# Twelve weight differences on GpSimd and four changes of order in the second attention group of a hybrid layer

## The chip, the core and the metric

The kernel runs on one core of a Trainium2 chip. The metric is the device time of one execution in microseconds (us). The engines are TensorE (PE, matmuls and transposes into PSUM), VectorE (DVE), ScalarE (ACT), GpSimd (POOL) and SyncE (SP, which here only issues DMAs). Each engine works its own queue in order; the queues meet through semaphores.

## What is computed

A layer over 1024 tokens of width 1024, in float32:

```
hn = rmsnorm(x);  proj = hn @ w_in                  # queries, keys, values of two groups
o_a = window attention, 8 query heads, 2 kv heads, |i-j| <= 128, a learned sink per head
o_b = neighbourhood attention on a 16 x 64 grid, 8 heads, window 8 x 16, learned bias
h  = x + concat(rmsnorm(o_a), rmsnorm(o_b)) @ w_out
hn = rmsnorm(h)
g  = conv3(hn @ w_gate) + conv_b;  u = hn @ w_up    # hidden width 2816
out = rmsnorm(h + (silu(g) * u) @ w_down)
```

## The kernel before, in words

**Arithmetic.** Every float32 operand of a matmul is split in two parts that TensorE takes at one pass each: a high part, made by an ACT copy, and a low part, the rest, made by a DVE subtraction. A product of a 128 x 128 weight block with 512 columns is then three matmuls: high x high, high x low, low x high (`block`, L168 to L171; `group`, L955 to L959). The weight halves are called whi and wlo, those of the probabilities ph and pl (`split_pt`, L413), those of activations hg.

**Order.** TensorE's order is written out by hand. For the other engines a scheduler takes instructions by priority, which is their place in the traced program, as far as their operands and buffers are ready in its own reckoning; the order in each queue is then fixed. `tc.high_priority(offset=n)` puts the instructions of a block n places forward. `behind(...)` (L145) keeps the instructions of a block, on the engine of the marked instruction, behind that instruction in its queue: it orders a queue and adds no wait between engines. Marks are kept in the dict `mark` and overwritten by each new instruction of that kind, so a mark means the latest one traced.

**Attention.** Projections are jobs m = 0 to 17 (`Project`, L554). They and the first half of the output projection (`OutA`, L590, eight tiles d of the four mixed tiles of group A) are fed as filler between the steps of attention units (`fill`, L805). A unit's step computes scores (L381), a softmax (L392: DVE adds the bias and takes the extreme, ACT the exp, DVE the reciprocal, POOL multiplies by it), transposes the probabilities on TensorE (pt), splits them into ph and pl and multiplies by the values (L528, L529). Group B's heads come last, and the last projection, m = 17, makes query and key of the last head. Its result is evacuated from PSUM by `evacuate` (L236, DVE), and `split_qk` (L292) makes ka on ACT and kb on DVE; four DMAs on SP then stack halves into q, kb and ka. `settle` (L725) calls this when the next job has run `LAG` = 3 blocks. `load` of the next job is traced when a job begins, `load_rest`, which makes the second half of a projection's weights, at its 12th block (`REST`). `OutA.run` first loads its tile xr of x (512 KB, SP, L604), which is added when the product leaves PSUM (L609). At the end of the attention units a dummy square root (L896) makes ACT load the table that later norms need.

**Gate and up.** Both products are computed with a Strassen-like scheme of seven products, each with its own weight combination: "11" and "12" are halves of the gate weights, "22" one of up, and s1, s2, s4, s3 are sums and differences: s1 = u1 + u2, s2 = s1 − g1, s4 = g2 − s2, s3 = g1 − u1. For the first four tiles (`HEAD` = 4, units 0 to 3, L1168 to L1217) each product is run for all four before the next: p1 and p2, p5 (s1), p6 (s2), p3 (s4), p7 (s3), p4 ("22"). Their weights are made by `head_weights` (L1000): it loads the raw weights it needs into one of three raw buffers (`load_raw`, L950, SP), forms the sum or difference into a buffer that the tile keeps through s1, s2, s4 and s3 (L998), and splits it into whi and wlo (`split_w`, L941, nine buffers each). The differences for s2, s4 and s3 go through `sub` (L996), a DVE subtraction. In the same stage DVE forms the activation combinations and their low parts (L996, L965), evacuates the products (L1108, L1115, L1119, L1132, L1137) and runs two taps of the convolution (L1126, L1127). From the fifth tile on a class `Weights` (L1043) makes the combinations, and its lines are not touched.

The parts that the change touches, and those that call them:

Of the kernel before, what the change touches and what calls it, by code (L numbers as in the profile page):

```python
# [30 lines left out]

LAG, LATE = 3, 13
FILL0, FILL1 = 22, 14
# [20 lines left out]
def hybrid_layer(tc, xT, w_first, w_in, w_out, w_gate, w_up, w_down, small, sink, rpb, consts, rope, out):  # L54
    nc = tc.nc
    with ExitStack() as ctx:
# [100 lines left out]

        def halve_w(raw):

            hi, lo = (wpool.tile([128, 4, 128], F32R, name=n, tag=n) for n in ("whi", "wlo"))  # L160
            mark["weights"] = nc.scalar.activation(hi, raw, AF.Copy)
            mark["weights low"] = nc.vector.tensor_tensor(lo, raw, f32(hi[:, :, :]), op=ALU.subtract)
            return [(hi[:, j, :], lo[:, j, :]) for j in range(4)]

        def load_w(src):
            return halve_w(fetch_w(src))

# [123 lines left out]

        def split_qk(t, urgent):  # L292

            a, b, q = big("ka", "op", F32R), big("kb", "op", F32R), big("q", "op", F32R)
            by = cst[:, K_SCALE:K_SCALE + 1]
            for h in range(2):
                with tc.high_priority(offset=urgent):
                    nc.scalar.activation(a[:, tsl(h)], t[:, tsl(h)], AF.Copy, scale=by)
                    nc.vector.scalar_tensor_tensor(b[:, tsl(h)], t[:, tsl(h)], by, f32(a[:, tsl(h)]), op0=ALU.mult, op1=ALU.subtract)
            with tc.high_priority(offset=500):  # L300
                nc.sync.dma_start(f32(q[0:64, :]), f32(a[0:64, :]))
                nc.sync.dma_start(f32(q[64:128, :]), f32(b[0:64, :]))
                nc.sync.dma_start(f32(b[0:64, :]), f32(a[64:128, :]))
                nc.sync.dma_start(f32(a[0:64, :]), f32(b[64:128, :]))
            return q, (a, b)
# [52 lines left out]
        def post(m, t):  # L358

            if m < 6:  # L360
                turn(m, t)
                stacks(m, t)
            else:
                hp, i = divmod(m - 6, 3)
                if i == 0:
                    vb[2 * hp], vb[2 * hp + 1] = split_v(t, (0, 1), lambda: done.add(m))
                else:
                    h = 2 * hp + i - 1
                    qb[h], kb[h] = split_qk(t, 500 * (m == 17))

# [21 lines left out]
        def softmax(st, j, ps, n, bias, nsink=None):  # L392
# [3 lines left out]
            with tc.high_priority(offset=50):  # L396
# [9 lines left out]
                e = n if nsink is None else n + 1  # L406
                mark["exp"] = nc.scalar.activation(p[:, j, 0:e], p[:, j, 0:e], AF.Exp, bias=nm, scale=-1.0, accum_out=sm[:, j:j + 1])  # L407
                if j == 1:
# [4 lines left out]
        def split_pt(ps, n):  # L413
            ph = apool.tile([128, HALF], F32R, name="ph", tag="ph")
            pl = apool.tile([128, HALF], F32R, name="pl", tag="pl")
            with tc.high_priority(offset=100):
                nc.scalar.activation(ph[:, 0:n], ps[:, 0:n], AF.Copy)  # L417
                nc.vector.tensor_tensor(pl[:, 0:n], ps[:, 0:n], f32(ph[:, 0:n]), op=ALU.subtract)  # L418
            return ph, pl
# [134 lines left out]
        class Project:  # L554
# [7 lines left out]
            def load_rest(self):  # L562
                self.w += halve_w(self.raw)

            def run(self):
# [7 lines left out]
                else:  # L573

                    ps = [bank("pj", "pj") for _ in range(2)]
                    for k in range(KT):
# [3 lines left out]
                        if k % 2:  # L580
                            mg[k // 2] = split(mix[k // 2], "mg", "xg")
                    for h in range(2):
                        evacuate(self.t, ps[h], h, self.grid)

# [5 lines left out]
        class OutA:  # L590
# [9 lines left out]
            def run(self):  # L600
                d = self.d
                h1[d] = big("h1", "mix" if d < 4 else "op")
                xt = tmp("xr")
                nc.sync.dma_start(xt, xT[d])  # L604
                for h in range(2):
                    ps = bank("pj", "pj")
                    yield from product(ps, self.w, mg[0:4], h)
                    with tc.high_priority(offset=500):
                        nc.vector.tensor_tensor(h1[d][:, tsl(h)], ps, xt[:, tsl(h)], op=ALU.add)  # L609
# [115 lines left out]
        def settle(age):  # L725

            for item in list(later):
                item[0] -= 1
                if item[0] <= 0:
                    later.remove(item)  # L730
                    item[1]()
            while waiting and (len(waiting) > 1 or age >= (LATE if waiting[0].m == 3 else LAG)):
                m = waiting[0].m
                if live["op"] + needs(m) > slots["op"]:
                    break
                live["op"] += needs(m)
                with behind(*["stack", "low"] * (m == 3)):
                    waiting.pop(0).post()
# [128 lines left out]
        for u in range(len(flat)):  # L867
# [26 lines left out]
            live["op"] -= 7 if u in (7, 15) else 4 if u >= 16 and u % 4 == 3 else 0  # L894
        with tc.high_priority(offset=500), behind("exp"):
            nc.scalar.activation(warm, eps, AF.Sqrt)  # L896
# [103 lines left out]
        def head_weights(i, name):  # L1000
# [4 lines left out]
            elif name == "s2":  # L1005
                g = load_raw(w_gate[f, :, 0:4], 4)
                sub(t, t, g)
            elif name == "s4":
                g = load_raw(w_gate[f, :, 4:8], 4)
                sub(t, g, t)  # L1010
            elif name == "s3":
                g, u = load_raw(w_gate[f, :, 0:4], 4), load_raw(w_up[f, :, 0:4], 4)
                sub(t, g, u)
            else:
# [550 lines left out]
```

## Time and profile before

| what | value |
|---|---|
| median of three runs | 1077.05 us (1076.45 to 1077.55) |
| the profiled execution's own time | 1077.36 us |
| its span, from the first to the last instruction | 1075.6 us |
| mean granted TensorE clock | 0.998 |
| instructions | 14910 |
| PE busy | 1063.6 us |
| DVE busy | 867.5 us |
| ACT busy | 554.9 us |
| POOL busy | 106.8 us |

The page has the busy time of each engine, the chain of work that ended last, and groups of instructions. The trace answers with the busy time in given stretches, with the instructions of an engine in order of time (start, duration, engine, line, operation, output <- inputs, and in brackets how long the engine was idle before and what ended that), and with groups of instructions of one shape. A matmul's record is longer than the step from one matmul to the next, because matmuls overlap. SPq and ACTq rows are the issuing of a DMA, not its transfer. The attention lasts to about 372 us, the second half of the output projection to about 434 us, the first four gate and up tiles to about 510 us, the other eighteen and the down projection to the end.

### The profile page before, as it was taken

The numbers are of one execution on the slowest core, as the hardware profiler recorded it, in microseconds if no ns is written. First come the engines' busy times: TensorE is split into PE (matmuls) and PEld (weight loads), VectorE is DVE, ScalarE is ACT, GpSimd is POOL, SyncE is SP. The second block draws the span as 40 slices with busy tenths as digits, with TensorE's granted clock in tenths as the row PEclk, the third lists the DMA queues.
The fourth block names the chain that finished last, engine by engine and source line by source line (L and its number), as shares of the span: only waits on it lengthen the run. The fifth ranks groups of instructions, "written<-read, shape, count | busy, mean of one in ns | idle before, by whom it ended". The sixth has DMA issues, their size and how long they took to land.

```text
span 1075.6 us, 14910 instructions
## 1 busy us (share of the span) xinstructions
PE 1063.6 (99%) x5094; PEld 889.3 (83%) x5094; DVE 867.5 (81%) x1596; ACT 554.9 (52%) x1059; POOL 106.8 (10%) x188
## 2 busy tenths in 40 slices
PE   9999999999999999999999999999999999999997
PEld 7888888888888888887788888888888888888887
DVE  7889887768888699899988877887887858987675
ACT  8457776647676545534534343442433646444451
POOL 0124332222342000000000000000000000000002
PEclk9999999999999999999999999999999999999999
DMA  7223122323235246214342232332222788766644
GB/s 278 73 74 82 38 69 60 89 69 82 75 87 159 83 152 216 79 48 158 145 159 97 96 121 79 128 107 109 98 89 98 246 293 304 269 223 219 230 153 157
DMA packets 68220, 144.94 MB, mean 135 GB/s; under 512 B 8240, under 2 KB 18736, under 8 KB 68144
## 3 DMA queue, kind: packets, MB, share of 16 engines
q1 hardware_dynamic: 57920, 118.69, 34.3%
q10 hardware_dynamic: 10224, 25.30, 6.2%
q8 instruction: 40, 0.66, 0.3%
q14 instruction: 36, 0.29, 0.1%
HBM read 103.58 MB, written 28.57 MB: 123 GB/s over the span
## 4 chain that ended last, share of the span: by engine, by line
PE 89%; DVE 8%; ACT 1%; DMA 1%; issue 1%; POOL 0%; DVEq 0%; ACTq 0%; SPq 0%; POOLq 0%
PE pj L169 8%; PE pj L170 7%; PE pj L171 7%; PE dn L957 7%; PE dn L959 7%; PE dn L958 7%; PE z L959 5%; PE z L957 5%; PE z L958 5%; PE s L381 3%; PE x L957 3%; PE x L958 3%; PE x L959 3%; PE y L959 3%; PE y L957 3%; PE y L958 3%
## 5 line engine op out<-in xcount | busy, mean ns | idle before, releaser
L946 ACT ACTIVATE whi<-ws 128x512 fp32r<-128x512 f32 (+1 forms) x100 | 60.3, 622 | 126.7 <-DVE ws L1064 82.5
L957 PE MATMUL dn<-xd,whi 128*128 128x512 f32 (+1 forms) x330 | 124.0, 376 | 0.0
L959 PE MATMUL dn<-xd,wlo 128*128 128x512 f32 (+1 forms) x330 | 123.7, 375 | 0.0
L958 PE MATMUL dn<-xd,whi 128*128 128x512 f32 (+1 forms) x330 | 123.7, 375 | 0.0
L959 PE MATMUL z<-hg,wlo 128*128 128x512 f32 x264 | 103.0, 390 | 0.7 <-DVE wlo L947 0.7
L169 PE MATMUL pj<-xgh,whi 128*128 128x512 f32 x245 | 103.2, 421 | 0.0
L957 PE MATMUL z<-hg,whi 128*128 128x512 f32 x264 | 103.0, 390 | 0.2 <-ACT whi L946 0.2
L958 PE MATMUL z<-hg,whi 128*128 128x512 f32 x264 | 102.7, 389 | 0.0
L407 ACT ACTIVATE p<-p,nm 128x385 f32<-128x385 f32 (+3 forms) x128 | 75.1, 587 | 49.3 <-DVE nm L403 48.4
L411 POOL TENSOR_SCALAR p<-p,sm 128x384 f32<-128x384 f32 (+1 forms) x128 | 79.5, 634 | 206.8 <-DVE sm L409 164.0
L171 PE MATMUL pj<-xgh,wlo 128*128 128x512 f32 x245 | 96.4, 393 | 0.0
L170 PE MATMUL pj<-xgl,whi 128*128 128x512 f32 x245 | 96.2, 393 | 0.0
L947 DVE TENSOR_TENSOR wlo<-raw,whi 128x512 fp32r<-128x512 f32 (+1 forms) x102 | 66.4, 672 | 26.1 <-ACT whi L946 25.0
L946 ACT ACTIVATE whi<-raw 128x512 fp32r<-128x512 f32 (+1 forms) x102 | 60.5, 612 | 46.0 <-DMA raw<-in_w_down_dram 19.6
L418 DVE TENSOR_TENSOR pl<-pt,ph 128x384 fp32r<-128x384 f32 (+2 forms) x108 | 63.5, 589 | 24.2 <-ACT ph L417 22.5
L947 DVE TENSOR_TENSOR wlo<-ws,whi 128x512 fp32r<-128x512 f32 (+1 forms) x100 | 67.0, 683 | 18.9 <-ACT whi L946 17.7
L1382 POOL TENSOR_TENSOR h<-h,wide 128x256 f32<-128x256 f32 (+1 forms) x6 | 5.4, 919 | 707.2 <-ACT wide L1378 707.2
L1272 ACT ACTIVATE xd<-xd 128x512 fp32r<-128x512 f32 x77 | 47.3, 626 | 47.6 <-DMA xd<-x 46.5
L959 PEld LDWEIGHTS dn<-xd,wlo 128*128 128x128 f32 x330 | 62.1, 188 | 11.2
L958 PEld LDWEIGHTS dn<-xd,whi 128*128 128x128 f32 x330 | 62.1, 188 | 11.1
L957 PEld LDWEIGHTS dn<-xd,whi 128*128 128x128 f32 x330 | 62.1, 188 | 11.1
L417 ACT ACTIVATE ph<-pt 128x384 fp32r<-128x384 f32 (+2 forms) x108 | 55.0, 512 | 30.7 <-PE pt L517 23.1
(270 smaller groups left out, 2675.8 us busy)
## 6 DMA issues: line engine op xcount, KB each, us to landing
xd<-x SPq DMA_DIRECT2D x77, 256.0 KB, 4.6
raw<-in_w_down_dram SPq DMA_DIRECT2D x72, 256.0 KB, 4.0
raw<-in_w_gate_dram SPq DMA_DIRECT2D x22, 512.0 KB, 3.6
raw<-in_w_up_dram SPq DMA_DIRECT2D x22, 512.0 KB, 4.3
x<-c ACTq DMA_DIRECT2D x22, 512.0 KB, 3.6
raw<-in_w_in_dram SPq DMA_DIRECT2D x30, 256.0 KB, 2.7
raw<-in_w_down_dram SPq DMA_DIRECT2D x36, 192.0 KB, 4.6
x<-t ACTq DMA_DIRECT2D x11, 512.0 KB, 2.7
```

The lines of the kernel that those rows point to most:

```text
L169: nc.tensor.matmul(ps, w[0], x[0][:, tsl(h)], start=first, stop=False)
L170: nc.tensor.matmul(ps, w[0], x[1][:, tsl(h)], start=False, stop=False)
L171: nc.tensor.matmul(ps, w[1], x[0][:, tsl(h)], start=False, stop=last)
L407: mark["exp"] = nc.scalar.activation(p[:, j, 0:e], p[:, j, 0:e], AF.Exp, bias=nm, scale=-1.0, accum_out=sm[:, j:j + 1])
L411: nc.gpsimd.tensor_scalar(p[:, i, 0:m], p[:, i, 0:m], sm[:, i:i + 1], 1.0, op0=ALU.mult, op1=ALU.mult)
L417: nc.scalar.activation(ph[:, 0:n], ps[:, 0:n], AF.Copy)
L418: nc.vector.tensor_tensor(pl[:, 0:n], ps[:, 0:n], f32(ph[:, 0:n]), op=ALU.subtract)
L946: nc.scalar.activation(hi, src, AF.Copy)
L947: nc.vector.tensor_tensor(lo, src, f32(hi[:, :, :]), op=ALU.subtract)
L957: nc.tensor.matmul(ps, w[0], x[0], start=first and i == 0, stop=False, skip_group_check=True)
L958: nc.tensor.matmul(ps, w[0], x[1], start=False, stop=False, skip_group_check=True)
L959: nc.tensor.matmul(ps, w[1], x[0], start=False, stop=last and i == len(ws) - 1, skip_group_check=True)
```

## The change

It has five parts. (1) `evacuate` of the last projection is raised by 500 places, `split_qk` of m = 17 is no longer raised, and the job is posted after 1 block of the next job in place of 3. (2) Weight halves made by `load_w` (the OutA tiles) and by `load_rest` of m = 17 are queued behind the latest traced ph (on ACT) and pl (on DVE). (3) The xr loads of OutA tiles 1 to 7 are queued on SP behind the third stacking DMA of the latest `split_qk`. (4) The dummy square root is queued behind the last ph in place of the last exp. (5) In `head_weights` the differences of s2, s4 and s3, four tiles each, are made by GpSimd in place of VectorE; the s1 sums, the splits and all of `Weights` stay.

```diff
-LAG, LATE = 3, 13
+LAG, LATE, SOON = 3, 13, 1
...
-        def halve_w(raw):
+        def halve_w(raw, held=False):
             hi, lo = (wpool.tile([128, 4, 128], F32R, name=n, tag=n) for n in ("whi", "wlo"))
-            mark["weights"] = nc.scalar.activation(hi, raw, AF.Copy)
-            mark["weights low"] = nc.vector.tensor_tensor(lo, raw, f32(hi[:, :, :]), op=ALU.subtract)
+            with behind(*["high", "rest"] * held):
+                mark["weights"] = nc.scalar.activation(hi, raw, AF.Copy)
+                mark["weights low"] = nc.vector.tensor_tensor(lo, raw, f32(hi[:, :, :]), op=ALU.subtract)
             return [(hi[:, j, :], lo[:, j, :]) for j in range(4)]
 
         def load_w(src):
-            return halve_w(fetch_w(src))
+            return halve_w(fetch_w(src), True)
...
-        def split_qk(t, urgent):
+        def split_qk(t):
...
             for h in range(2):
-                with tc.high_priority(offset=urgent):
-                    nc.scalar.activation(a[:, tsl(h)], t[:, tsl(h)], AF.Copy, scale=by)
-                    nc.vector.scalar_tensor_tensor(b[:, tsl(h)], t[:, tsl(h)], by, f32(a[:, tsl(h)]), op0=ALU.mult, op1=ALU.subtract)
+                nc.scalar.activation(a[:, tsl(h)], t[:, tsl(h)], AF.Copy, scale=by)
+                nc.vector.scalar_tensor_tensor(b[:, tsl(h)], t[:, tsl(h)], by, f32(a[:, tsl(h)]), op0=ALU.mult, op1=ALU.subtract)
             with tc.high_priority(offset=500):
                 nc.sync.dma_start(f32(q[0:64, :]), f32(a[0:64, :]))
                 nc.sync.dma_start(f32(q[64:128, :]), f32(b[0:64, :]))
-                nc.sync.dma_start(f32(b[0:64, :]), f32(a[64:128, :]))
+                mark["stacked"] = nc.sync.dma_start(f32(b[0:64, :]), f32(a[64:128, :]))
                 nc.sync.dma_start(f32(a[0:64, :]), f32(b[64:128, :]))
...
-                    qb[h], kb[h] = split_qk(t, 500 * (m == 17))
+                    qb[h], kb[h] = split_qk(t)
...
-                mark["exp"] = nc.scalar.activation(p[:, j, 0:e], ...)
+                nc.scalar.activation(p[:, j, 0:e], ...)
...
-                nc.scalar.activation(ph[:, 0:n], ps[:, 0:n], AF.Copy)
-                nc.vector.tensor_tensor(pl[:, 0:n], ps[:, 0:n], f32(ph[:, 0:n]), op=ALU.subtract)
+                mark["high"] = nc.scalar.activation(ph[:, 0:n], ps[:, 0:n], AF.Copy)
+                mark["rest"] = nc.vector.tensor_tensor(pl[:, 0:n], ps[:, 0:n], f32(ph[:, 0:n]), op=ALU.subtract)
...
             def load_rest(self):
-                self.w += halve_w(self.raw)
+                self.w += halve_w(self.raw, self.m == 17)
...
-                    for h in range(2):
-                        evacuate(self.t, ps[h], h, self.grid)
+                    with tc.high_priority(offset=500):
+                        for h in range(2):
+                            evacuate(self.t, ps[h], h, self.grid)
...
-                nc.sync.dma_start(xt, xT[d])
+                with behind(*["stacked"] * (d > 0)):
+                    nc.sync.dma_start(xt, xT[d])
...
-            while waiting and (len(waiting) > 1 or age >= (LATE if waiting[0].m == 3 else LAG)):
+            while waiting and (len(waiting) > 1 or age >= (LATE if waiting[0].m == 3 else SOON if waiting[0].m == 17 else LAG)):
...
-        with tc.high_priority(offset=500), behind("exp"):
+        with tc.high_priority(offset=500), behind("high"):
             nc.scalar.activation(warm, eps, AF.Sqrt)
...
             elif name == "s2":
                 g = load_raw(w_gate[f, :, 0:4], 4)
-                sub(t, t, g)
+                nc.gpsimd.tensor_tensor(t, t, g, op=ALU.subtract)
             elif name == "s4":
                 g = load_raw(w_gate[f, :, 4:8], 4)
-                sub(t, g, t)
+                nc.gpsimd.tensor_tensor(t, g, t, op=ALU.subtract)
             elif name == "s3":
                 g, u = load_raw(w_gate[f, :, 0:4], 4), load_raw(w_up[f, :, 0:4], 4)
-                sub(t, g, u)
+                nc.gpsimd.tensor_tensor(t, g, u, op=ALU.subtract)
```

More of the change, by code (lines that the diff above doesn't have):

```diff
@@ L406, in softmax @@
                 e = n if nsink is None else n + 1
-                mark["exp"] = nc.scalar.activation(p[:, j, 0:e], p[:, j, 0:e], AF.Exp, bias=nm, scale=-1.0, accum_out=sm[:, j:j + 1])
+                nc.scalar.activation(p[:, j, 0:e], p[:, j, 0:e], AF.Exp, bias=nm, scale=-1.0, accum_out=sm[:, j:j + 1])
                 if j == 1:
```

## The prediction

> **What bounds the kernel now.** I read the page's first and fourth parts first, then busy time by stretch, then TensorE's timeline for the places where it really stands still.
>
> ```profile
> PE 1063.6 (99%) x5094; PEld 889.3 (83%) x5094; DVE 867.5 (81%) x1596; ACT 554.9 (52%) x1059; POOL 106.8 (10%) x188
> PE 89%; DVE 8%; ACT 1%; DMA 1%; issue 1%; POOL 0%; DVEq 0%; ACTq 0%; SPq 0%; POOLq 0%
> ```
>
> TensorE (PE) is the bound: it is busy in 1063.6 us of the 1075.6 us span, and the chain of waits lies on it for 89%. So a change away from TensorE can only win back moments in which TensorE waits, and there are few. The 8% of the chain on VectorE (DVE) matter, since they lie in one place. The rows below are stretches of time: length, then busy time (with instructions) of PE, weight loads, DVE, ACT, POOL, then clock, DMA share and GB/s.
>
> ```profile
> 450.00:500.00 50.00, 49.47 (x217) 40.04 (x216) 48.90 (x78) 23.97 (x38) 0.00 (x0) 1.00 0.21 69
> 500.00:525.00 25.00, 24.42 (x106) 19.39 (x105) 23.96 (x32) 11.58 (x16) 0.00 (x0) 1.00 0.50 186
> 550.00:575.00 25.00, 25.00 (x112) 20.71 (x111) 22.11 (x33) 11.29 (x18) 0.00 (x0) 1.00 0.37 131
> ```
>
> In the steady stage (550 to 575) TensorE runs 112 matmuls in 25 us, one per 0.22 us. From 450 to 525, the stage of the first four gate and up tiles, DVE is busy 48.90 of 50 and 23.96 of 25 us and POOL does nothing at all. TensorE's waits between its start-up and its last stage are these rows (start, duration, instruction, and in brackets idle time and releaser):
>
> ```profile
> 286.56 0.44 PE L529 MATMUL o<-pl,v 128*128 128x384 f32 x1 [0.86 <-DVE pl L418]
> 329.60 0.39 PE L529 MATMUL o<-pl,v 128*128 128x256 f32 x1 [0.88 <-DVE pl L418]
> 338.49 0.39 PE L381 MATMUL s<-kb,q 128*128 128x256 f32 x1 [0.32 <-DMA kb<-ka]
> 360.17 0.44 PE L529 MATMUL o<-pl,v 128*128 128x384 f32 x1 [0.15 <-DVE pl L418]
> 495.83 0.50 PE L957 MATMUL z<-hg,whi 128*128 128x512 f32 x1 [0.19 <-ACT whi L946]
> 496.90 0.50 PE L959 MATMUL z<-hg,wlo 128*128 128x512 f32 x1 [0.34 <-DVE wlo L947]
> 513.69 0.50 PE L959 MATMUL y<-hg,wlo 128*128 128x512 f32 x1 [0.18 <-DVE wlo L947]
> 517.28 0.50 PE L959 MATMUL z<-hg,wlo 128*128 128x512 f32 x1 [0.40 <-DVE wlo L947]
> 531.44 0.50 PE L959 MATMUL y<-hg,wlo 128*128 128x512 f32 x1 [0.28 <-DVE wlo L947]
> ```
>
> A bracket understates the loss, since a matmul's record (0.39 us for an undisturbed one, as the 499.30 row below) outlasts its 0.22 us step. I add 0.16 to each. The wait at 286.56 lies before everything that the change traces differently, and I leave it. The three of group B's attention are then 1.04 + 0.48 + 0.31 = **1.83 us**. The five of the gate and up stage are 0.35 + 0.50 + 0.34 + 0.56 + 0.44 = **2.19 us**. Together 4.0 us is all that this change can win.
>
> **The attention edits.** Those around the last projection (m = 17) and the first output tiles meet the waits at 329.60 and 338.49. First ACT, then DVE:
>
> ```profile
> 325.11 0.62 ACT L161 ACTIVATE whi<-raw 128x512 fp32r<-128x512 f32 x1
> 325.63 1.32 ACT L298 ACTIVATE ka<-t,cst 128x512 fp32r<-128x512 f32 x2
> 326.86 0.63 ACT L417 ACTIVATE ph<-pt 128x256 fp32r<-128x256 f32 x2
> ...
> 324.30 0.69 DVE L242 TENSOR_TENSOR t<-pj,rstd 128x512 f32<-128x512 f32 x1
> 326.63 1.98 DVE L299 SCALAR_TENSOR_TENSOR kb<-t,cst,ka 128x512 fp32r<-128x512 f32 x2
> 329.13 0.74 DVE L418 TENSOR_TENSOR pl<-pt,ph 128x256 fp32r<-128x256 f32 x2
> ```
>
> The split of the probabilities (ph, then pl) stands behind a weight conversion of 0.62 us and two urgent ka of 1.32 on ACT, then behind two urgent kb of 1.98 on DVE. That makes pl 1 us late. Without the urgency ph and pl (raised by 100) go ahead of ka and kb, and the held weight halves no longer step in front of ph. TensorE's 1.04 should go. The price is a later ka and kb. It is met by the evacuation at 324.30, which stood in DVE's queue (its row names no releaser) and is now raised by 500, and by posting at age 1 in place of 3, which brings the splits two blocks of three matmuls forward in the trace, 1.3 us of TensorE's steps. I set these against each other at nothing; without them the split is late by about that much, and the kb scores are next to be late. Holding the weights costs nothing that I see: a tile's halves are made within the job before (8 blocks of three matmuls, 5.4 us at least).
>
> The transfers, SyncE's queue and then the reader of xr:
>
> ```profile
> 326.78 0.33 SPq L604 DMA_DIRECT2D xr<-in_xT_dram  x1
> ...
> 328.64 0.47 SPq L302 DMA_DIRECT2D q<-kb  x1
> 329.15 0.77 SPq L604 DMA_DIRECT2D xr<-in_xT_dram  x1
> ...
> 333.41 0.46 SPq L303 DMA_DIRECT2D kb<-ka  x1
> ...
> 336.72 0.69 DVE L609 TENSOR_TENSOR h<-pj,xr 128x512 f32<-128x512 f32 x1
> ```
>
> ```profile
> raw<-in_w_gate_dram SPq DMA_DIRECT2D x22, 512.0 KB, 3.6
> ```
>
> kb<-ka overwrites what q<-kb reads, so it starts 4.8 us behind it, while two xr loads of 512 KB cross. Both xr now queue behind kb<-ka. Without them q<-kb should land sooner and the 0.48 at 338.49 go. In return the first xr starts at 333.9 at the latest; with the 3.6 us of the other 512 KB loads it lands at 337.5, 0.8 us after L609 wants it. With q<-kb faster by a us it is in time. Between 0 and 0.8 I take **0.3**, as pl behind L609 has some room.
>
> ```profile
> 357.64 1.28 ACT L896 ACT_TABLE_LOAD   x1
> ...
> 359.05 0.85 ACT L417 ACTIVATE ph<-pt 128x384 fp32r<-128x384 f32 x2
> ```
>
> The table load of 1.28 us stands between the last exp and the last ph. Behind the last ph it meets only a weight conversion that isn't due, and the 0.31 at 360.17 goes. The attention comes to −1.83 + 0.30 = **−1.53 us**.
>
> **The twelve differences.** First POOL and DVE groups (busy, mean ns), then a collision, POOL and DVE; then two groups of DVE from 466 to 497 and one, the s2 differences, from 430 to 445:
>
> ```profile
> L1382 POOL TENSOR_TENSOR h<-h,wide 128x512 f32<-128x512 f32 x2 | 2.6, 1294 | 692.1 <-ACT wide L1378 692.1
> ...
> L996 DVE TENSOR_TENSOR ws<-raw 128x512 f32<-128x512 f32 x4 | 2.8, 691 | 0.4 <-DMA raw<-in_w_up_dram 0.4
> ...
> 247.97 0.99 POOL L481 TENSOR_TENSOR xb<-cst,rr 128x384 f32<-128x384 f32 x1 [1.18 <-DVE nm L403]
> 248.01 1.50 DVE L162 TENSOR_TENSOR wlo<-raw,whi 128x512 fp32r<-128x512 f32 x1
> ...
> L1115 DVE TENSOR_TENSOR gs<-z,c 128x512 f32<-128x512 f32 x4 | 2.8, 691 | 0.0
> L1119 DVE TENSOR_TENSOR gs<-y,gs 128x512 f32<-128x512 f32 x4 | 2.8, 691 | 0.0
> ...
> L996 DVE TENSOR_TENSOR ws<-ws,raw 128x512 f32<-128x512 f32 x4 | 2.7, 687 | 0.0
> ```
>
> On POOL such an instruction takes 1.29 us, on DVE 0.69. It is not simply off DVE's back: in the collision DVE's subtraction of two SBUF operands, 0.69 elsewhere, took 1.50, as if it had waited out POOL's 0.99. The Trainium skill ("SBUF — State Buffer", Who interferes with whom) states it as a lock: a DVE instruction with two SBUF inputs and a POOL instruction that reads SBUF exclude each other, and the second waits for the whole of the first. The row agrees with it; the rival below is its full price.
>
> The four s2 differences lie before the full stretch, and I price only the eight of s4 and s3. DVE's readers of PSUM have one SBUF operand and should stay free of POOL: from 466 to 497 the gs groups are 5.6 of 31 us, with the fewer of c about a quarter (my estimate). A POOL difference thus holds DVE for about 0.75 × 1.29 = 0.97 us and takes 0.69 off it: DVE comes out 0.28 **later**, 2.2 us for eight. (Bounds: nothing locked, 5.5 us earlier; all locked, 4.8 us later.)
>
> What the move buys is order.
>
> ```profile
> 490.94 0.33 SPq L952 DMA_DIRECT2D raw<-in_w_up_dram  x1
> ...
> 494.36 0.69 DVE L996 TENSOR_TENSOR ws<-raw 128x512 f32<-128x512 f32 x1 [0.44 <-DMA raw<-in_w_up_dram]
> 496.76 0.69 DVE L947 TENSOR_TENSOR wlo<-raw,whi 128x512 fp32r<-128x512 f32 x1
> ...
> 510.01 0.69 DVE L1064 TENSOR_TENSOR ws<-raw 128x512 f32<-128x512 f32 x1
> ...
> 499.30 0.39 PE L957 MATMUL z<-hg,whi 128*128 128x512 f32 x1
> ```
>
> A raw buffer comes free only when the difference that reads it has had its turn in DVE's full queue; the last s3 difference waited for a load issued at 490.94, made DVE idle for 0.44 and TensorE for 0.85 (495.83, 496.90). POOL's queue holds nothing else in this stage, so nothing is held up behind a waiting difference there; the s4 differences run as soon as their operands are there and not at DVE's turn, and the loads of s3 and "22" follow sooner. The 0.60 us that each takes longer is paid by ACT's high half, which waits for it. I count the 0.85 as gone. What is late next is the first "22" low half: done at 497.45, wanted by the third matmul from 499.30, 499.75, which is 498.9 with the 0.85 gone, so 1.45 of room. DVE's lag of 2.2 less the 0.44 is 1.8: **0.35 late**. Of the other 1.34 (513.69, 517.28, 531.44) I take half, **0.67**: the weights of tile four can be loaded sooner, but its s1 sum at 510.01 is also placed by DVE's order, which stays full. Stage: −0.85 + 0.35 − 0.67 = −1.17.
>
> Sum: −1.53 − 1.17 = −2.70 us. The profiled execution took 1077.36 (its span 1075.6 and 1.8 around it), 0.3 above the median of 1077.05; on the median this is **1074.4**.
>
> **Rivals.** (a) *The order buys nothing in the gate and up stage.* For it: DVE is full whoever subtracts; against: the 0.44 wait on the load. Attention alone: 1077.05 − 1.53 = 1075.5. (b) *A wait takes the place of the one removed in attention*: ka and kb, no longer urgent, slip a us and the kb scores wait 1 us longer in place of 0.48 less. Attention is then −1.53 + 1.48 = −0.05, the whole −1.2: 1075.8. For it: 338.49 already waits; against: the two xr out of the way. (c) *The lock decides, slower.* All twelve differences hold DVE for the full 1.29 inside its full stretch: 12 × 0.60 = 7.2 us of lag, less 0.44 and 1.45 of room, 5.3 late on TensorE; with −0.85 and −1.53 that is +2.9: 1080.0. It decides from a lag of about 6.5 us; for it the 1.50 row, against it the readers of PSUM and the room before 444. By the skill's lock this is the case whenever POOL's turns meet only two-operand work. (d) The change could simply re-deal the static order of the later stages; that is no more than a us or two either way, as TensorE doesn't wait anywhere from 532 to 1049.
>
> **How the numbers follow.** Forecast (both halves pay, 1072.9 to 1075.0): 0.52. (a) 0.16, (b) 0.12, (c) 0.13, (d) and the rest 0.07. Low end: all 4.0 us, 1073.0, and 0.4 of luck: 1072.6. High end: (a) and (b) with 3 us of lag besides, 1079.0; it leaves out (c). A measurement here tells about 0.2% (2.15 us) from no change: faster is below 1074.9, slower above 1079.2. Faster 0.54, the same 0.31, slower 0.15.
>
> **What would show it.** Right: no waits at L529 near 329 and 360 or at L381 near 338; the table load behind the last ph; both xr behind kb<-ka; the twelve differences as POOL rows near 1.3 us, the last of s3 before 491 where DVE had it at 494.36; no wait near 496. Wrong: L609 waiting for xr; DVE records of 1 to 2 us beside POOL's differences; a new TensorE wait between 465 and 500, for a low half or for "22".

## The result, and the profile after

The change makes the kernel **slower**: 1080.26 us (1079.93 to 1084.05, nine runs) against 1077.13 us (1076.35 to 1078.16, nine runs of the kernel before beside them). The ratio is 1.0035, with a 95% interval of 1.0026 to 1.0043. The profiled execution took 1079.98 us, with a span of 1078.1 us and a mean clock of 0.996. Behind L160 line numbers are one or two higher than before: the low half of a weight is L949, the high half L948, c<-x L1100, c<-y L1110, GpSimd's differences L1009 (s2), L1012 (s4), L1015 (s3).

The page of the changed kernel, busy time and chain:

```profile
PE 1062.9 (99%) x5094; PEld 890.1 (83%) x5094; DVE 865.7 (80%) x1584; ACT 555.6 (52%) x1059; POOL 125.2 (12%) x200
PE 88%; DVE 6%; DMA 2%; ACT 2%; issue 1%; POOL 1%; DVEq 0%; SPq 0%; ACTq 0%; POOLq 0%
```

Twelve instructions have gone from DVE to POOL (1596 to 1584, 188 to 200), each 0.69 us long on DVE, but DVE's busy time fell by only 1.8 us. Most of what they left came back inside other instructions. TensorE's timeline of the changed kernel, first at the places of the attention where it now pauses, then its three waits with a bracket between 286 and the last stage:

```profile
303.03 0.38 PE L517 MATMUL pt<-cst,p 128*128 128x128 f32 x2
303.48 0.44 PE L528 MATMUL o<-ph,v 128*128 128x384 f32 x1
304.07 0.44 PE L529 MATMUL o<-pl,v 128*128 128x384 f32 x1
...
497.12 0.50 PE L961 MATMUL z<-hg,wlo 128*128 128x512 f32 x1 [0.68 <-DVE wlo L949]
518.03 0.50 PE L959 MATMUL x<-hg,whi 128*128 128x512 f32 x1 [2.01 <-ACT c L1100]
523.78 0.79 PE L959 MATMUL y<-hg,whi 128*128 128x512 f32 x1 [2.69 <-DVE c L1110]
```

The eight waits that the prediction added up are gone. There is one that it named, for the "22" low half (497.12), and two that it did not, of 2.16 and 2.85 us when a step of 0.23 is taken off the distance from one matmul's start to the next. TensorE's order is the same in both kernels, so their timelines can be laid side by side. The changed kernel reaches the wait at 286.56 at 285.61; that 0.95 lies before all that the change traces differently. From there to the first matmul behind the attention's last norm (373.97, 371.84) it is 1.18 us shorter; from that to the first product of gate and up tile five (510.18, 507.70) another 0.35; from that to the first product of tile six (527.82, 530.74) **5.40 longer**; from there to the sums at the end (1067.80, 1070.34) 0.38 shorter. The whole loss lies in one tile.

ACT and DVE of the changed kernel just there, then the same two evacuations before:

```profile
516.37 0.61 ACT L948 ACTIVATE whi<-ws 128x512 fp32r<-128x512 f32 x1
516.89 0.61 ACT L948 ACTIVATE whi<-raw 128x512 fp32r<-128x512 f32 x1
517.41 0.57 ACT L1100 ACTIVATE c<-x 128x512 f32<-128x512 f32 x1
...
520.10 0.69 DVE L949 TENSOR_TENSOR wlo<-ws,whi 128x512 fp32r<-128x512 f32 x1
520.70 1.29 DVE L949 TENSOR_TENSOR wlo<-raw,whi 128x512 fp32r<-128x512 f32 x2
521.90 1.22 DVE L1140 TENSOR_TENSOR c<-c,cv 128x1024 f32<-128x1024 f32 x1
523.04 0.69 DVE L1110 TENSOR_TENSOR c<-y,c 128x512 f32<-128x512 f32 x1
```

```profile
513.13 0.60 ACT L1098 ACTIVATE c<-x 128x512 f32<-128x512 f32 x1 [0.56 <-PE x L959]
518.95 0.69 DVE L1108 TENSOR_TENSOR c<-y,c 128x512 f32<-128x512 f32 x1
```

TensorE has issued the first product of tile five by 510.42. Its next product into that bank waits until ACT has evacuated it (c<-x), which comes at 517.41, behind weights; before, ACT stood ready for it at 513.13. The same with c<-y on DVE at 523.04; before, it ran at 518.95. So the two evacuations of tile five are late. DVE's queue is also another one: from the reciprocal of the stage's norm (440.07; 442.38 before) up to c<-y it holds 107 instructions in place of 110, though eight differences have left it. Five that stood behind c<-y now stand ahead of it, four low halves and a c<-c,cv. After the longer pause TensorE also runs slower (length, then busy time of PE, weight loads, DVE, ACT, POOL, then the granted clock):

```profile
521.00:523.70 2.70, 0.09 (x1) 0.00 (x0) 2.70 (x5) 0.51 (x2) 0.00 (x0) 0.94 0.46 158
523.70:526.00 2.30, 2.22 (x5) 1.82 (x6) 2.27 (x5) 0.42 (x1) 0.00 (x0) 0.50 0.73 289
526.00:528.00 2.00, 2.00 (x8) 1.59 (x7) 1.46 (x3) 0.20 (x1) 0.00 (x0) 0.81 0.50 193
528.00:531.00 3.00, 3.00 (x15) 2.48 (x14) 2.75 (x5) 1.80 (x3) 0.00 (x0) 1.00 0.36 139
```

The twelve matmuls from 523.78 take 4.24 us in place of 2.72: 1.5 us more. With the two waits that is 6.5, less the 0.90 of the old waits at 513.69 and 517.28: about the 5.40.

What made DVE late? Groups of DVE from 440 to 500, the changed kernel first, then before (busy, mean ns, idle before):

```profile
L967 DVE TENSOR_TENSOR hg<-h,hg 128x512 fp32r<-128x512 f32 x20 | 15.1, 788 | 0.7 <-ACT hg L966 0.6
L949 DVE TENSOR_TENSOR wlo<-ws,whi 128x512 fp32r<-128x512 f32 x12 | 9.3, 788 | 3.9 <-ACT whi L948 3.9
L1129 DVE SCALAR_TENSOR_TENSOR cv<-gs,par,cv 128x1023 f32<-128x1023 f32 x2 | 3.0, 1498 | 0.0
```

```profile
L965 DVE TENSOR_TENSOR hg<-h,hg 128x512 fp32r<-128x512 f32 x20 | 13.0, 691 | 0.2 <-ACT hg L964 0.2
L947 DVE TENSOR_TENSOR wlo<-ws,whi 128x512 fp32r<-128x512 f32 x12 | 8.1, 689 | 1.2 <-PE sw L232 1.2
```

Two things. The same instructions on two SBUF operands are 0.1 us longer in the mean (2.1 + 1.2 us, and 0.4 for a tap of the convolution, 1281 ns before). And DVE, whose low halves of these weights waited only at the norm (1.2 us), now waits 3.9 us for high halves: 1.4 at the norm and 2.47 in front of one s3 low half. There the high half on ACT waits for a difference on POOL, and that waits for its load (two of POOL's four s3 differences, then ACT and DVE behind the first):

```profile
481.76 1.28 POOL L1015 TENSOR_TENSOR ws<-raw 128x512 f32<-128x512 f32 x1 [3.45 <-DMA raw<-in_w_up_dram]
485.86 1.52 POOL L1015 TENSOR_TENSOR ws<-raw 128x512 f32<-128x512 f32 x1 [2.82 <-DMA raw<-in_w_up_dram]
...
483.07 0.63 ACT L948 ACTIVATE whi<-ws 128x512 fp32r<-128x512 f32 x1 [4.09 <-POOL ws L1015]
...
483.73 0.69 DVE L949 TENSOR_TENSOR wlo<-ws,whi 128x512 fp32r<-128x512 f32 x1 [2.47 <-ACT whi L948]
```

From this I had two theories. **Lock**: GpSimd's reads of SBUF hold up DVE, and what DVE does late in this stage TensorE pays. **Order**: the lock is small change; the loss is that weights which the scheduler reckons ready sooner now stand in front of the evacuations.

### The profile page after: what moved, and what is told of

It is laid out like the page before. It is cut to its first block, busy times and chain, and to the rows that moved or that the text cites. A ratio compares the mean times of both kernels' runs of the same rounds, so it can differ in the third digit from the quotient of the medians.

```text
span 1078.1 us, 14915 instructions
## 1 busy us (share of the span) xinstructions
PE 1062.9 (99%) x5094; PEld 890.1 (83%) x5094; DVE 865.7 (80%) x1584; ACT 555.6 (52%) x1059; POOL 125.2 (12%) x200
## 4 chain that ended last, share of the span: by engine, by line
PE 88%; DVE 6%; DMA 2%; ACT 2%; issue 1%; POOL 1%; DVEq 0%; SPq 0%; ACTq 0%; POOLq 0%
PE pj L170 8%; PE pj L172 8%; PE pj L171 8%; PE dn L959 7%; PE dn L960 7%; PE dn L961 7%; PE z L959 4%; PE z L960 4%; PE z L961 4%; PE s L381 3%; PE x L959 3%; PE x L960 3%; PE x L961 3%; PE y L959 3%; PE y L960 3%; PE y L961 3%
## 5 line engine op out<-in xcount | busy, mean ns | idle before, releaser
L948 ACT ACTIVATE whi<-ws 128x512 fp32r<-128x512 f32 (+1 forms) x100 | 60.5, 623 | 144.6 <-DVE ws L1066 86.4
L949 DVE TENSOR_TENSOR wlo<-raw,whi 128x512 fp32r<-128x512 f32 (+1 forms) x102 | 66.3, 672 | 30.8 <-ACT whi L948 28.3
L949 DVE TENSOR_TENSOR wlo<-ws,whi 128x512 fp32r<-128x512 f32 (+1 forms) x100 | 68.3, 694 | 22.1 <-ACT whi L948 22.0
L948 ACT ACTIVATE whi<-raw 128x512 fp32r<-128x512 f32 (+1 forms) x102 | 60.7, 612 | 44.6 <-DMA raw<-in_w_down_dram 21.5
L959 PE MATMUL y<-hg,whi 128*128 128x512 f32 x176 | 69.2, 393 | 2.7 <-DVE c L1110 2.7
```

What stands on the lines that cost most here:

```text
L948: nc.scalar.activation(hi, src, AF.Copy)
L949: nc.vector.tensor_tensor(lo, src, f32(hi[:, :, :]), op=ALU.subtract)
L959: nc.tensor.matmul(ps, w[0], x[0], start=first and i == 0, stop=False, skip_group_check=True)
```

## The experiments

All times are medians of five to twelve runs; the difference is to the kernel before, run beside each.

| kernel | us | difference | ratio, 95% interval |
|---|---|---|---|
| e1_attention: attention edits alone | 1076.53 | −0.24 | 0.9999 [0.9990, 1.0008] |
| e2_gpsimd: the twelve differences alone | 1082.25 | +5.48 | 1.0048 [1.0035, 1.0061] |
| e5_dummy: e1 and twelve useless reads | 1082.46 | +5.69 | 1.0052 [1.0040, 1.0064] |
| e7_behind: change, weights behind evacuations | 1078.87 | +2.10 | 1.0019 [1.0010, 1.0027] |
| e3_raised: change, evacuations raised | 1079.85 | +2.70 | 1.0022 [1.0013, 1.0031] |
| e8_s3only: e1 and the four s3 on GpSimd | 1080.86 | +3.71 | 1.0030 [1.0019, 1.0041] |
| e9_memset: change, twelve fills | 1072.99 | −4.16 | 0.9959 [0.9947, 0.9971] |
| e11_self: change, twelve self-additions | 1077.53 | +0.66 | 1.0004 [0.9994, 1.0015] |
| e16_s3self: change, s3 as self-additions | 1077.77 | +0.80 | 1.0009 [1.0000, 1.0018] |
| e10_less: e1 less hold and table edit | 1075.98 | −1.17 | 0.9986 [0.9978, 0.9995] |
| e17_table: e1 less hold | 1075.24 | −1.73 | 0.9983 [0.9974, 0.9992] |
| e12_s2: e10 and the four s2 on GpSimd | 1075.57 | −1.30 | 0.9988 [0.9979, 0.9996] |

**The two halves of the change.** First the attention edits alone, the changed kernel with:

```diff
-                nc.gpsimd.tensor_tensor(t, t, g, op=ALU.subtract)
+                sub(t, t, g)
...
-                nc.gpsimd.tensor_tensor(t, g, t, op=ALU.subtract)
+                sub(t, g, t)
...
-                nc.gpsimd.tensor_tensor(t, g, u, op=ALU.subtract)
+                sub(t, g, u)
```

> Only the four attention edits; the twelve differences stay on VectorE. Order theory (the loss comes from tile five's weights standing ahead of its evacuations in the queues of ACT and DVE, once GpSimd has let them get ready sooner) and lock theory (the loss comes from GpSimd holding DVE's second SBUF port): the waits at 329, 338 and 360 us go, the five of the gate and up stage stay: 1077.1 - 1.9 = 1075.2. If the attention edits themselves lose: 1077 or more.

Then the same three lines the other way round, in the kernel before (e2_gpsimd):

> Only the twelve differences on GpSimd; attention as before. Order theory and lock theory alike: the result without the 1.9 us that attention won, 1080.3 + 1.9 = 1082.2, with two TensorE waits over 2 us near 520. If the loss needs TensorE's earlier arrival from attention as well: 1077 to 1079.

The attention edits gained 0.24 us, within the noise, though TensorE's waits at 329, 338 and 360 are gone in their trace as well. The differences alone cost 5.48 us, and their trace has the same waits for the evacuations of tile five as the changed kernel's, without any of the attention edits:

```profile
520.71 0.50 PE L957 MATMUL x<-hg,whi 128*128 128x512 f32 x1 [1.84 <-ACT c L1098]
526.46 0.50 PE L957 MATMUL y<-hg,whi 128*128 128x512 f32 x1 [2.71 <-DVE c L1108]
```

So the loss is made by the differences alone. The halves don't add up, though: −0.24 and +5.48 make +5.24 and not +3.13. The differences alone have two waits more, of 0.69 at 417 (for the norm's v) and 0.84 at 437 (for c<-x), which the changed kernel's trace lacks; why the attention edits take them away is open.

**GpSimd's reads without any change of order.** e5_dummy keeps the differences on DVE and adds, after the split of each s2, s4 and s3, a subtraction of the low half from itself on GpSimd into a mask that nothing reads any more (lo is the low half as 128 x 512). It leaves out nothing. The line is written shorter here.

```diff
             W[f, name] = split_w(t, 4)
+            if name in ("s2", "s4", "s3"): nc.gpsimd.tensor_tensor(cst[:, K_MB:K_MB + 512], lo, lo, op=ALU.subtract)
```

> As e1_attention, and GpSimd does twelve useless subtractions of the same size besides (the low half of each s2, s4 and s3 weight set minus itself, into a dead mask), so that the lock is there and the order of DVE and ACT is not changed. Lock theory: DVE late by 12 x 0.4 to 1.0 us, 1078 to 1083. Order theory: DVE records stretched by some 5 us in all, but no wait over 2 us of TensorE near 520: 1075.2 to 1076.5.

It costs 5.93 us against e1_attention. TensorE's waits of it in the stage:

```profile
486.23 0.50 PE L959 MATMUL z<-hg,whi 128*128 128x512 f32 x1 [0.56 <-ACT whi L948]
487.97 0.50 PE L961 MATMUL z<-hg,wlo 128*128 128x512 f32 x1 [1.00 <-DVE wlo L949]
492.11 0.50 PE L959 MATMUL z<-hg,whi 128*128 128x512 f32 x1 [1.58 <-ACT whi L948]
494.14 0.79 PE L961 MATMUL z<-hg,wlo 128*128 128x512 f32 x1 [1.29 <-DVE wlo L949]
```

DVE's own instructions and their order are those of e1_attention, no instruction of DVE or ACT waits for POOL in the stage, and yet DVE is late with low halves: its busy time over the whole kernel is 873.6 us for 867.3. The lock exists and is dear; the order theory alone falls.

**Is it then the order at all?** e7_behind makes tile five's weights s4, s3 and "22" only after its evacuations (`behind("cx", "cy")`, marks on c<-x and c<-y, and fewer early steps of the weights):

```diff
+            with behind("cx", "cy"):
+                mine.step(9)
```

> The changed kernel, all twelve on GpSimd, with tile five's s4, s3 and 22 weights traced after its p1 and p5 and queued behind their evacuations. Order theory: the waits of 2.2 and 2.9 us and the low clock after them (1.5 us) go for the most part: 1074.5 to 1077. Lock theory: as the changed kernel, 1079 to 1080.5.

e3_raised raises the two evacuations and moves nothing else:

```diff
-                nc.scalar.activation(self.c[:, 0:HALF], self.x, AF.Copy)
+                with tc.high_priority(offset=400 * (self.f == FO[HEAD])): nc.scalar.activation(self.c[:, 0:HALF], self.x, AF.Copy)
...
-                nc.vector.tensor_tensor(self.c[:, HALF:S], self.y, self.c[:, 0:HALF], op=ALU.add)
+                with tc.high_priority(offset=400 * (self.f == FO[HEAD])): nc.vector.tensor_tensor(self.c[:, HALF:S], self.y, self.c[:, 0:HALF], op=ALU.add)
```

> The changed kernel with two instructions of tile five raised by 400 places: the evacuations of its first and fifth product, c<-x on ACT and c<-y on DVE (L1100, L1110). In the queues this puts c<-y ahead of three low halves and one product with cv, and c<-x ahead of one more high half; nothing else moves. Order theory (the loss is that these two stand behind weights that became ready early): the waits of 2.16 at 518.03 and 2.85 at 523.78 and the clock's drop behind them go, the weights are up to 1 us late instead, 1075.5 to 1077.5. Lock theory (DVE has as much work as before, so whatever stands last is late): the low halves are 2 us and more late in place of the evacuations, no more than 1.5 us better than the changed kernel, 1078.7 to 1080.

They came 1.0 and 0.4 us nearer to before than the change. e7_behind lies between the two ranges that it was given, 0.1 below the lock theory's; e3_raised lies in the lock theory's. TensorE's waits in e3_raised:

```profile
519.34 0.50 PE L959 MATMUL x<-hg,whi 128*128 128x512 f32 x1 [1.42 <-ACT c L1100]
522.65 0.50 PE L959 MATMUL y<-hg,whi 128*128 128x512 f32 x1 [0.31 <-DVE c L1110]
526.79 0.50 PE L959 MATMUL z<-hg,whi 128*128 128x512 f32 x1 [1.12 <-DVE gs L1117]
536.04 0.50 PE L959 MATMUL z<-hg,whi 128*128 128x512 f32 x1 [0.80 <-DVE c L1134]
```

The wait for c<-y fell from 2.69 to 0.31, and the two evacuations behind it (gs, then c) became late in its place. DVE is behind; the order only says who waits. That is the lock theory's picture.

**The same order without reads, and with them.** In e9_memset each of the twelve is a fill that reads nothing; in e11_self it adds the buffer to itself. Both leave out the differences and so do not compute the layer. One of the three lines is shown:

```diff
-                nc.gpsimd.tensor_tensor(t, t, g, op=ALU.subtract)
+                nc.gpsimd.memset(t, 0.001)                            # e9_memset
+                nc.gpsimd.tensor_tensor(t, t, t, op=ALU.add)          # e11_self
```

> The changed kernel with the twelve GpSimd subtractions replaced by twelve GpSimd fills with a constant, which read nothing (the combinations s2, s4 and s3 of the first four tiles are left out and their weights are a constant). DVE keeps all that the change took off it, and GpSimd reads nothing beside it; from 500 on ACT's and DVE's queues keep the changed kernel's order. Lock theory: DVE's stretched records go, DVE is about 5 us ahead by 500, the waits at 518 and 523 shrink to under 0.5 us each: 1074 to 1076. Order theory: with the same queues the waits at 518 and 523 stay at 1.5 us or more each, because the weights ahead of the evacuations wait for loads and not for DVE's time: 1078 to 1080.

> The twin of the kernel with twelve fills: in place of each fill GpSimd adds the buffer to itself (s2, s4 and s3 of the first four tiles are left out and hold multiples of s1). All other engines' queues and every DMA are the same as with the fills, and the loads that the differences read are waited for by nothing in either; only GpSimd's instruction differs, which now reads SBUF and takes 1.3 us in place of 0.53. Lock theory (the 7.3 us between the changed kernel and the fills are DVE standing still beside GpSimd's reads): 1079 to 1082. Load theory (the fills gained because no difference had to wait for its raw weights): 1073 to 1074.5, as the fills.

The fills give 1072.99 us, 7.3 below the change and below the ranges of both theories. TensorE has no wait over 0.25 from 373 to the last stage; c<-y runs at 517.21 and its reader at 518.43. The self-additions give 1077.53. DVE and POOL groups from 440 to 500 of the fills, then DVE's of the self-additions with the one long wait that came back:

```profile
L967 DVE TENSOR_TENSOR hg<-h,hg 128x512 fp32r<-128x512 f32 x20 | 12.9, 685 | 0.1
L949 DVE TENSOR_TENSOR wlo<-ws,whi 128x512 fp32r<-128x512 f32 x13 | 8.6, 684 | 1.6 <-ACT whi L948 1.6
...
L1015 POOL MEMSET ws<- 128x512 f32 x4 | 2.1, 528 | 10.8 <-DVE wlo L949 10.7
```

```profile
L967 DVE TENSOR_TENSOR hg<-h,hg 128x512 fp32r<-128x512 f32 x20 | 15.7, 819 | 0.1
L949 DVE TENSOR_TENSOR wlo<-ws,whi 128x512 fp32r<-128x512 f32 x12 | 9.1, 784 | 1.4 <-ACT whi L948 1.4
...
522.07 0.54 PE L959 MATMUL y<-hg,whi 128*128 128x512 f32 x1 [2.72 <-DVE c L1110]
```

With the same order on DVE and ACT, DVE's means go from 685 to 819 ns and from 684 to 784, 2.7 + 1.2 us, DVE's idle time from 440 up to c<-y is about the same (4.8 and 4.7 us), and c<-y runs at 521.33, 4.1 us later. TensorE pays this with the one pause, 2.88 us by its steps, and with 1.7 us of slower matmuls behind it. The fills have the changed kernel's 107 instructions ahead of c<-y too, so that queue by itself makes nothing late. Against before the two kernels stand 4.8 us apart (−4.16, +0.66): the price of twelve GpSimd instructions that read. A part of it could be that a self-addition takes 1.25 to 1.40 us where the fill takes 0.53; but the 3.9 us of stretch make up nearly all of the 4.1. The Trainium skill ("SBUF — State Buffer", Who interferes with whom) makes this very distinction: a DVE instruction with two SBUF inputs contends with a GpSimd instruction that reads SBUF, and not with one that only writes it. These rows agree.

The pages of e1_attention, the fills and the changed kernel (above) give DVE's account as a whole; first e1_attention's, then the fills':

```profile
PE 1062.6 (99%) x5094; PEld 888.7 (83%) x5094; DVE 867.3 (81%) x1596; ACT 555.9 (52%) x1059; POOL 106.5 (10%) x188
```

```profile
PE 1061.5 (99%) x5094; PEld 890.0 (83%) x5094; DVE 860.1 (80%) x1584; ACT 555.0 (52%) x1059; POOL 113.0 (11%) x200
```

The move takes 7.2 us off DVE (867.3 to 860.1), and reading puts 5.6 of them back (865.7 in the changed kernel).

But the lock is not all either: 1077.53 lies below the range that the lock theory gave, and is not 1080.26.

**The rest of the loss.** e8_s3only and e16_s3self look for it in s3, whose differences need two loads each. e16_s3self leaves s3 out and does not compute the layer.

```diff
-                sub(t, g, u)                                          # e8_s3only, in e1_attention
+                nc.gpsimd.tensor_tensor(t, g, u, op=ALU.subtract)
...
-                nc.gpsimd.tensor_tensor(t, g, u, op=ALU.subtract)     # e16_s3self, in the changed kernel
+                nc.gpsimd.tensor_tensor(t, t, t, op=ALU.add)
```

> The changed kernel with the s2 and s4 differences back on DVE: only the four of s3 on GpSimd, besides the attention edits. Lock theory alone: four collisions cost about a third of twelve (0.44 each by the stretched records), less a third of the work taken off: nothing to +0.5 beside the attention edits alone. Order theory: the early weights come from the s4 and s3 buffers freed early; in ACT's queue the evacuation c<-x now stands ahead of two high halves, so the wait at 518 goes, and the result is that of the attention edits alone, 1076 to 1077.5. If both were wrong and the loss came from the s3 chain, it would be 1079 or more.

> The changed kernel with only the four s3 differences replaced by the buffer added to itself (s3 of the first four tiles is left out and holds a multiple of an earlier combination); s2 and s4 are made as in the changed kernel. GpSimd still makes twelve instructions that read SBUF, but the s3 ones wait for no load; DVE's and ACT's queues are those of the kernel with all twelve self-additions. If the 2.7 us between that kernel (1077.5) and the changed one (1080.3) are DVE waiting for s3's weights, whose differences wait for their loads: 1077 to 1078. If they lie in where the s2 and s4 differences collide with DVE: 1079.5 to 1080.5.

Four s3 differences alone cost as much as all twelve: neither theory said so; the third guess on record, that the loss comes from the s3 chain, did. Their trace shows why, and that of e16_s3self shows it gone (DVE's low halves from 440 to 500, first e8_s3only):

```profile
L949 DVE TENSOR_TENSOR wlo<-ws,whi 128x512 fp32r<-128x512 f32 x12 | 8.1, 684 | 6.9 <-ACT whi L948 5.8 <-PE sw L233 1.1
```

```profile
L949 DVE TENSOR_TENSOR wlo<-ws,whi 128x512 fp32r<-128x512 f32 x12 | 9.3, 802 | 1.4 <-ACT whi L948 1.4
```

With s3 on GpSimd the low half's place in DVE's queue moves forward, as if s3 came early; but its loads come no sooner, and DVE stands still for 5.8 us in front of three of the four. With s3 that waits for no load (e16_s3self) those waits are gone (the 1.4 left is the norm's), the lock's stretch is all there (802 ns), and the time is +0.80, 2.3 us below the change. What remains there is the lock: as in e11_self, to which it differs only by s2 and s4.

**A place where the lock is free.** e12_s2 moves the four s2 differences alone, in the kernel with the better attention edits.

```diff
-                sub(t, t, g)
+                nc.gpsimd.tensor_tensor(t, t, g, op=ALU.subtract)
```

> The two better attention edits (1075.98 by themselves) with the four s2 differences alone on GpSimd. In the queues this takes four instructions out of DVE's between about 414 and 430 us and moves nothing else. Place theory (the lock costs only where DVE is full, after 444): nothing lost, nothing won, 1075.5 to 1076.5. Number theory (each collision costs the end about 0.5 us wherever it stands): four cost 1.5 to 2.5, 1077.5 to 1078.5. The kernel with the s3 differences alone came out at 1080.86 with no fewer than four, so a place with its own price is the likelier.

1075.57 beside 1075.98, inside each other's intervals: nothing lost, nothing won. Collisions are there (DVE, an activation sum of 0.69 and two low halves of 1.29 elsewhere):

```profile
425.38 1.77 DVE L984 TENSOR_TENSOR s<-s,s 128x512 f32<-128x512 f32 x1
...
429.65 2.18 DVE L967 TENSOR_TENSOR hg<-h,hg 128x512 fp32r<-128x512 f32 x2
```

They cost TensorE one new wait of 0.41 at 435.44, and from 495 to 530 its waits are those of e10_less again. In this place, with DVE busy for 27.5 of the 30 us from 410 to 440, four collisions cost nothing that shows; that the other eight bear the whole price of reading is an inference, as no run has those of s4 and s3 alone.

**The attention.** e10_less takes two parts back from the attention edits, e17_table only the first of them.

```diff
-                self.w += halve_w(self.raw, self.m == 17)
+                self.w += halve_w(self.raw, False)
...
-        with tc.high_priority(offset=500), behind("high"):            # e10_less only
+        with tc.high_priority(offset=500), behind("exp"):
```

> The attention edits alone, less two of their parts: the second weight half of the last projection is not held behind ph and pl, and the table load stays behind the last exp. My theory is that the first of these brought the new waits at 303 (0.33 and 0.42) by letting two exps and two ph run together, and the second the longer ones at 371 (0.27 and 0.53 for 0.34) by moving DVE's order of the norm, against 0.43 taken away at 360. Then: no wait at 303, 0.43 back at 360, 0.34 at 373, 0.7 us shorter up to 373 than the attention edits alone, 1075.5 to 1076. The rival: the waits at 303 and 371 belong to the earlier posting of the last projection, and stay: 1076.5 to 1077.

> The attention edits alone, less the hold on the second weight half of the last projection; the table load stands behind the last ph, as in the changed kernel. By the two traces at hand the hold costs 0.33 and 0.42 at 303, the table load's move gains 0.43 at 360 and loses 0.27 and 0.19 at 371: 1075.7 to 1076.2, the same as without the table load's move (1075.98), with the waits of 371 and without those of 303 and 360. If the move was worth its 0.43: 1075.5 with 371 as before.

Without the hold the pauses at 303 (0.34 and 0.42 in the changed kernel) are gone in both. In ACT's queue the held high half stood between ph and the next exps, which then ran in a pair, with two ph behind them in a pair, and TensorE waited for the pair. The table load's move took 0.43 at 360 and gave back 0.46 at 371 (0.27 and 0.53 for 0.34): e10_less and e17_table differ by less than their intervals. The hold thus cost about 1.5 us by the medians (−0.24 against −1.73; the two intervals just touch), of which the traces show about 0.7 at 303, and 0.65 of a wait at 1040.55 that e1_attention has and e17_table lacks (e10_less has 0.33 of it, so the hold is not its only cause). e17_table, 1075.24 us, has the lowest median of those that compute the layer, though not clear of e10_less and e12_s2: it beats the kernel before and the changed one.

## Why the prediction was wrong, step by step

The forecast was 1074.4 us, and its range ended at 1079.0. Against before, the measured +3.1 is −0.24 (attention) −3.9 (what a DVE freed at no price is worth: e9_memset less e1_attention) +4.8 (reads: e11_self less e9_memset) +2.5 (differences that wait for loads, 2.3 of it s3's by e16_s3self: change less e11_self). By their intervals each of the last three is good to about 1.5 us. Against the attention edits alone the differences thus lose 0.9 by collisions, net of the work that DVE is rid of, and 2.5 by their loads.

- **"All that this change can win" is 4.0 us.** About right: the fills, which remove all the waits that I had counted and keep the new pauses at 303 and 371, gained 4.16.
- **Attention −1.53.** The three waits went, and xr cost nothing of its 0.30: kb<-ka was issued 3.1 us behind q<-kb in place of 4.8, and no L611 waits for a load. But **"Holding the weights costs nothing that I see" failed**: for the second half of m = 17 it cost about 1.5 us by medians whose intervals just touch, and about 0.7 of it can be seen at 303. The table load's move was costed at nothing too, and gave back what it won. I looked at what the held conversions wait for, and not at what then runs in their place.
- **DVE 0.28 later per difference, 2.2 for eight.** The sum was about right, by luck. A collision stretched DVE by less than the 0.97 that I took: in the groups from 440 to 500 3.7 us for eight, 0.46 each, less than the 0.60 that a difference takes off (7.2 for twelve; I had taken the 0.69 of its record), so that each left DVE *earlier* by itself. Instead DVE stood idle 4.0 us more between the reciprocal and c<-y (7.3 for 3.3), mostly for halves whose inputs came late: 2.47 in front of the s3 low half, 1.9 in front of low halves of raw weights at 500 and 502, 0.7 at a convolution tap. Off 4.8, back 3.7 and 4.0: 2.9 later. The five instructions that moved ahead of c<-y add about 3.5, which makes the 6.4 that this stretch of DVE is longer (82.97 for 76.57).
- **The order: "the loads of s3 and '22' follow sooner".** The last s3 difference did end at 487.4, 7.7 us sooner than before, and the 0.85 at 496 went. But "nothing is held up behind a waiting difference" was only true of POOL's queue: DVE's low halves had moved forward with it, and one waited for 2.47 us.
- **"What is late next is the first '22' low half ... 0.35 late". This is the step that failed.** It was late, by 0.84 at 497.12, and cost no more than the waits that went. But I carried the lag no further than to "22". About 20 us later the evacuations of tile five stood behind weights in the queues that the change had re-dealt (I had not asked what comes to stand ahead of them), and there the lag cost TensorE 2.16 and 2.85, and 1.5 of clock. All of the 1.34 that I had halved was won, and did not matter.
- **Rival (c), "The lock decides", 1080.0.** Its sign and its place (DVE's full stretch) were right, and its number by accident: it priced a full 0.60 of lag on each of twelve and let s3's loads cost nothing. It said that it decides from 6.5 us of lag; 2.9 were enough, since with the new queue c<-y has hardly any room (e9_memset: it ends at 517.89 and is wanted at 518.43).

## What to carry to other kernels

Moving an elementwise instruction from DVE to GpSimd hardly frees DVE where GpSimd reads SBUF beside DVE instructions with two SBUF operands: here twelve of them took 7.2 us off DVE and put 5.6 back as longer instructions, and twelve that did not read were worth 4.8 us more than twelve that did. In a stage where DVE had some room, four cost nothing, but won nothing either. When an engine falls behind by 2 or 3 us, follow that lag down its queue to the evacuations that free a PSUM bank, and not only to the next operand; and when an input is made earlier on another engine, check that its load comes earlier too, since its reader's place in a static queue will.

## What the runs showed of the hardware

TensorE's granted clock fell to 0.50 for 2.3 us behind the pause of 2.69 us, as the windows of the changed kernel show; e11_self, whose stage has no other pause, has the same behind its 2.72 (0.58 from 522 to 524.4, 0.56 to 526). The changed kernel's pause of 2.01 left it at 1.00 (518 to 521), and so did one of 1.40 (e8_s3only) and 1.42, 0.31 and 1.12 within 8 us (e3_raised), but four pauses of 0.56 to 1.58 within 8 us (e5_dummy) brought it down too:

```profile
491.00:493.00 2.00, 0.74 (x2) 0.30 (x2) 2.00 (x3) 1.58 (x3) 0.00 (x0) 1.00 0.66 231
493.00:495.00 2.00, 0.86 (x2) 0.77 (x3) 2.00 (x4) 1.43 (x2) 0.77 (x1) 0.64 0.01 5
495.00:497.00 2.00, 2.00 (x6) 1.52 (x6) 2.00 (x4) 0.67 (x2) 0.71 (x2) 0.51 0.58 161
```

So a pause of 2.7 us in TensorE cost about half as much again behind it: the twelve matmuls there took 1.5 us more in the changed kernel, 1.7 in e11_self. The Trainium skill ("TensorE: Matmul & The Clock Gate", HAM oscillation — how this bites in real kernels) gives as its abstract rule "no PE-idle gaps >~3.4µs". By that rule the 2.7 us would do no harm; here they did, and the measurement decides.
